# Two column groups of 384 instead of 512 and 256 for the products over all 768 tokens

## Chip, cores, metric

One core of one Trainium2 chip runs the kernel. The metric is the device time of one execution in microseconds; several executions are timed and the median is quoted.

## What is computed

A backbone of two layers over 512 latent tokens and 256 context tokens, model width 1024, in float32. Each layer runs three token mixers side by side (multi-head latent attention "MLA", a bidirectional gated linear recurrence "HGRN2", differential attention), merges them, and ends with a SwiGLU feed-forward network. The first layer computes all of it for all 768 tokens; the second needs from the context only what the latent tokens read of it.

```python
for l in range(2):
    ctx_out = l < 1
    h = x * (1 + sc1) + sh1                      # the same for ctx
    p = h @ w_in[l]                              # queries, keys, values, gates of all mixers
    y = (mla(p), hgrn2(p), diff_attention(p))    # latent tokens read context and latent tokens
    m = sum(sigmoid(h @ w_gate[i] + b_gate[i]) * (y[i] @ w_branch[i]) for i in range(3))
    x = post_norm(x, g1 * (m @ w_o))
    h2 = x * (1 + sc2) + sh2
    x = post_norm(x, g2 * ((silu(h2 @ w1a) * (h2 @ w1b)) @ w_ff2))
    # for ctx the same again, in the first layer only
```

## The kernel before

**Products.** Activations lie with features on the partitions and tokens along the free axis, split into a high and a low part (`h[0]`, `h[1]`); a weight tile of 128 output features is loaded, split the same way (`split_w`, line 380: ACT copies the high part `wh`, DVE subtracts for the low part `wl`), and each product is made of three matmuls per block of 128 input features (`mm3`, line 482): `wh`·`h` high, `wh`·`h` low, `wl`·`h` high. `fm_groups` (line 495) does this for a list of column groups `(offset, width)`: for each group it takes one PSUM bank, runs through the blocks, and calls `evac`, which brings the bank to SBUF. `GX = (256, 512)` are the latent tokens, `GC = (0, 256)` the context; a product over all 768 tokens runs GX and then GC. For a weight with 8 blocks that is 24 matmuls of 512 columns and 24 of 256.

**Jobs.** Such a product of one weight tile is a job. `win_jobs` (line 990) makes the 32 jobs per layer of the input projection (names dq, dk, dv of the differential attention, ff, fb, hq, hi, hg of the recurrence), `merge_jobs` (line 1557) the 8 gates and 8 branch products of each mixer, `ff1_jobs` (line 1778) the 44 products of the FFN's first half. Jobs stand in one list and run in its order. A job of the branch products waits for its mixer and for the differential attention (`Need(f"y{l}_2")` in `bran`).

**Order of the work.** The order of every engine's instructions is fixed when the program is built. The attentions and the recurrence are chains of short steps on PE, ACT and DVE (`mla` line 1016, `diff` line 1163, `hgrn` line 1374). `weave` (line 453) lays them between the jobs: where a chain yields `At(t)`, the time at which its next input will be ready by the cost table in `Clock.note` (line 199), it puts steps of the current job in front, until its count of PE's time has come near `t`. A step is six matmuls (two blocks of input features) of one group. In the first layer that list begins, beside the mixers, with the input projection and six gates of the first merge (lag 6 in `merge_jobs`); the first branch product can't be placed before the differential attention has ended. In the second layer it is the same.

**Tiles of names.** `b` and `S` are PSUM tiles (one bank, two banks), `wh`, `wl` and `wr` the split and the raw weights, `h` the activations, `s` and `k` tiles of 768 columns (the mixers' operands among them), `ident` the identity for transposes, `colv` columns of biases and gains, `ac` the FFN's gate.

```python
    def fm_groups(self, wt, nk, rhs, groups, evac, m=P, needs=None):
        for gi, (o, n) in enumerate(groups):
            if needs:
                yield Need(needs[gi])
            ps = self.bank()
            for k in range(nk):
                lh, ll = wt(k)
                rh, rl = rhs(k, o, n)
                self.mm3(ps[:m, :n], lh, ll, rh, rl, k == 0, k == nk - 1)
                if k % 2 == 1 and k != nk - 1:
                    yield 6 * mmcost(n)
            evac(ps, o, n)
            yield (6 if nk % 2 == 0 else 3) * mmcost(n)

```

Of the kernel before, what the change touches and what calls it, by code (L numbers as in the profile page):

```python
# [19 lines left out]
NK = 8  # L20
TX, TC, T = 512, 256, 768
XO = TC
# [10 lines left out]
MODJ = 2  # L33
O_HQ, O_FF, O_FB, O_HI, O_HG, O_DQ, O_DK, O_DV = 416, 928, 1440, 1952, 2464, 2976, 3488, 4000
GX, GC = (XO, TX), (0, TC)
XT = [2, 3, 4, 5]
CT = [0, 1]

# [231 lines left out]
class Kern:  # L270
# [529 lines left out]
    def mod_half(self, key, t, xo, g, hx, eng):  # L800
        nc = self.nc
        cx = 0 if t in XT else 1
        A, B = self.ab[key]
# [37 lines left out]
    def b1_tile(self, l, t):  # L841
        nc = self.nc
        first = not self.b1q
        isx = t in XT
        c0 = 0 if (isx or l == 0) else 256
# [144 lines left out]
    def win_jobs(self, l, names):  # L990

        nc = self.nc
        offs = dict(hq=O_HQ, ff=O_FF, fb=O_FB, hi=O_HI, hg=O_HG, dq=O_DQ, dk=O_DK, dv=O_DV)
        for nmj, j in names:
            ctxn = l == 0 or nmj in ("ff", "fb", "hi", "dk", "dv")
            groups = [GX, GC] if ctxn else [GX]
            park = self.dram([P, T])
            self.win[nmj, j] = park
            w = self.I["w_in"][l][:, offs[nmj] + j * P: offs[nmj] + (j + 1) * P]

            def body(job, nmj=nmj, j=j, groups=groups, park=park, ctxn=ctxn):
                s = self.slab()

                def evac(ps, o, n):
                    if o == XO:
                        nc.scalar.copy(s[:, o:o + n], ps[:, :n])
                    else:
                        nc.vector.tensor_copy(s[:, o:o + n], ps[:, :n])
                yield from self.fm_body(NK, self.hrhs(self.h), groups, evac, needs=[f"hx{l}", f"hc{l}"])(job)
                o = 0 if ctxn else XO  # L1010
                nc.sync.dma_start(park[:, o:], s[:, o:])
                self.done.add(f"win{l}_{nmj}{j}")
            self.add(Job(body, self.load_fm(w, NK), 1024))


    def mla(self, l):
# [6 lines left out]
        for h in range(8):  # L1023
            tiles += [(h, t, 6) for t in XT]
            if l == 0:
# [137 lines left out]
    def diff(self, l):  # L1163
# [3 lines left out]
        for h in range(4):  # L1167
            tiles += [(h, t, 6) for t in XT]
            if l == 0:
# [387 lines left out]
    def merge_jobs(self, l, br, seq):  # L1557
        nc, I = self.nc, self.I
        o0 = 0 if l == 0 else XO
        groups = [GX, GC] if l == 0 else [GX]  # L1560
        st = {}

        gates, brans = [], []
# [214 lines left out]
    def ff1_jobs(self, l):  # L1778
        nc, I = self.nc, self.I
        full = l == 0  # L1780
        groups = [GX, GC] if full else [GX]
        first = groups if full else [(XO, 256), (XO + 256, 256)]
        needs = [f"h2x{l}", f"h2c{l}"] if full else [f"h2a{l}", f"h2x{l}"]
        self.act = [None] * NFF
        every, self.every = self.every, 0
        for j in range(NFF):
            if j == MODJ:
                self.every, self.tick = every, 0.0
            st = {}

            def gate(job, j=j, st=st):
                def evac(ps, o, n):
                    st["g", o] = self.fp.tile([P, TX], F32, tag="ac", bufs=4, name=self.nm("ac"))
                    nc.scalar.activation(st["g", o][:, :n], ps[:, :n], AF.Silu)
                if j == 0:
                    st["late"] = self.fm_body(NK, self.hrhs2, first[1:], evac, needs=needs[1:])(job)
                yield from self.fm_body(NK, self.hrhs2, groups if j else first[:1], evac, needs=None if j else needs)(job)

            def up(job, j=j, st=st):
                a = self.slab()  # L1800
                self.act[j] = a

                def evac(ps, o, n):
                    nc.vector.tensor_tensor(a[:, o:o + n], st["g", o][:, :n], ps[:, :n], ALU.mult)
                if "late" in st:
                    job.defer = True
                    yield from self.fm_body(NK, self.hrhs2, first[:1], evac)(job)
                    yield from st["late"]
                    yield from self.fm_body(NK, self.hrhs2, first[1:], evac)(job)
                else:  # L1810
                    yield from self.fm_body(NK, self.hrhs2, groups, evac)(job)
                if j == NFF - 1:
                    self.done.add(f"act{l}")
            w = I["w_ff1"][l]
            self.add(Job(gate, self.load_fm(w[:, j * P:(j + 1) * P], NK), 1024))
            self.add(Job(up, self.load_fm(w[:, FF + j * P:FF + (j + 1) * P], NK), 1024))
# [24 lines left out]
def build(ctx, tc, I, out):  # L1841
# [4 lines left out]
    for t in range(6):  # L1846
        res[t] = I["ctx"][0, t * P:(t + 1) * P] if t < 2 else I["x"][0, (t - 2) * P:(t - 1) * P]
    order = XT + CT

# [9 lines left out]
    def start0(xin):  # L1859
# [3 lines left out]
        for g in range(2):  # L1863
            for blk in ((2, 0), (3, 1))[g]:
                yield Need(f"mod0_{blk}")
            for i, t in enumerate(XT):
                hx = K.fp.tile([P, TX], F32, tag="ac", bufs=4, name=K.nm("ac"))
# [178 lines left out]
```

## Time and profile before

| | |
|---|---|
| median of 3 runs | 2987.1 us (2985.87 to 2991.09) |
| profiled execution | 2997.48 us |
| its span, first to last instruction | 2995.7 us |
| mean granted TensorE clock | 0.964 of full speed |
| busy: PE, DVE, ACT, POOL | 2759.8, 1729.5, 1271.7, 273.0 us |

The span is the profiled execution's; the profiled execution as a whole took 0.35% longer than the median. Busy time of PE counts a matmul from its start to a modelled end, and matmuls overlap: what one costs in a dense stretch is the distance from its start to the next one's start, which the timeline gives. On a timeline row an instruction that is repeated without a gap stands once, with its count behind the x; in brackets stands how long the engine was idle before it and what ended that.

The stages: the first layer's MLA runs from about 160 to 445 us, its differential attention to 734, its recurrence to 980, the rest of the merge to 1080, the output projection and a normalisation to 1220, the FFN's first half to 1570, its second half, a normalisation and the second layer's first products to 1877; the second layer's MLA to 2092, its differential attention to 2293, its recurrence and merge to 2530, its FFN to the end.

### The profile page before, as it was taken

The page shows a single profiled execution, that of the slowest core. Times are in us where ns is not written, and L with a number is a line of the kernel's source. Part 1 is how long each engine was busy: PE and PEld are TensorE (multiplying, and loading weights), DVE is VectorE, ACT ScalarE, POOL GpSimd, SP SyncE. Part 2 cuts the span into 40 slices and gives each one's busy share as a digit, 9 for nine tenths or more (in the row PEclk, how much of TensorE's full clock was granted, in tenths as well). Part 3 has the DMA queues.
Part 4 walks back from the last instruction along what each step waited for, and adds up shares of the span by engine and source line. Part 5 has one row for each costly group of instructions (what it writes and reads, how often), then busy time and mean ns, then how long its engine had stood idle before and what let it go on. Part 6 is the DMA issues. An engine that isn't in the chain of part 4 may idle for free. (4 is left out here: it accounts for less than half of the span.)

```text
span 2995.7 us, 38612 instructions
## 1 busy us (share of the span) xinstructions
PE 2759.8 (92%) x14899; PEld 2327.7 (78%) x14899; DVE 1729.5 (58%) x2776; ACT 1271.7 (42%) x2321; POOL 273.0 (9%) x223
## 2 busy tenths in 40 slices
PE   6999989887999996999999989999989998799997
PEld 2888777766888885888888767888877887688875
DVE  4566656655876267555543566665665766622235
ACT  3545545576333224334432355444555453322222
POOL 1000000000000004333320120000000000300002
PEclk8999999988999998999999999999999999799998
DMA  6333353422432354353433354323332543333331
GB/s 216 99 115 93 110 150 125 139 62 86 139 121 90 106 188 132 121 155 118 150 105 120 106 184 112 93 89 120 106 110 85 174 129 132 115 99 99 106 127 70
DMA packets 345519, 359.11 MB, mean 120 GB/s; under 512 B 31114, under 2 KB 263044, under 8 KB 345336
## 3 DMA queue, kind: packets, MB, share of 16 engines
q1 hardware_dynamic: 343144, 351.84, 37.4%
q10 hardware_dynamic: 1680, 4.42, 0.4%
q8 instruction: 117, 1.92, 0.3%
q14 instruction: 66, 0.54, 0.1%
q0 software_dynamic: 512, 0.39, 0.0%
HBM read 298.10 MB, written 58.49 MB: 119 GB/s over the span
## 5 line engine op out<-in xcount | busy, mean ns | idle before, releaser
L106 PE MATMUL b<-h,wh 128*128 128x512 f32 (+1 forms) x5152 | 1372.9, 355 | 52.8 <-DVE h L106 15.3
L106 PEld LDWEIGHTS b<-h,wh 128*128 128x128 f32 x5152 | 905.9, 192 | 185.0 <-DVE h L106 16.4
L106 PE MATMUL b<-h,wl 128*128 128x512 f32 (+1 forms) x2576 | 905.9, 352 | 0.0
L106 DVE TENSOR_TENSOR wl<-wr,wh 128x1024 fp32r<-128x1024 f32 (+1 forms) x384 | 478.1, 1250 | 603.3 <-ACT wh L106 602.4
L106 ACT CAST wh<-wr 128x1024 fp32r<-128x1024 f32 (+1 forms) x384 | 379.8, 995 | 419.1 <-PE b L106 326.8
L106 PEld LDWEIGHTS b<-h,wl 128*128 128x128 f32 x2576 | 493.3, 191 | 65.1
L106 POOL TENSOR_TENSOR sm<-sm,mhalf 128x1 f32<-128x1 f32 (+3 forms) x80 | 56.4, 705 | 2439.6 <-DVE sm L106 2439.6
L106 ACT ACTIVATE s<-S,sm 128x768 f32<-128x768 f32 (+1 forms) x170 | 135.4, 797 | 336.2 <-DVE sm L106 288.9
L106 PE MATMUL S<-wh,ac 128*128 128x512 f32 x512 | 174.0, 404 | 17.5 <-DVE ac L106 11.5
L106 PE MATMUL b<-ident,s 128*128 128x128 f32 (+3 forms) x687 | 111.5, 277 | 70.4 <-ACT s L106 28.4
L106 PE MATMUL b<-k,wh 128*128 128x512 f32 (+1 forms) x576 | 165.4, 375 | 9.8 <-ACT k L106 9.1
L106 DVE TENSOR_TENSOR k<-b,k 128x512 fp32r<-128x512 f32 (+1 forms) x136 | 84.9, 627 | 134.7 <-ACT k L106 134.6
L106 PEld LDWEIGHTS b<-ident,s 128*128 128x128 f32 (+3 forms) x687 | 81.3, 142 | 92.9 <-ACT s L106 37.0
L106 PE MATMUL S<-k,k 96*128 96x512 f32 (+2 forms) x576 | 137.3, 341 | 12.6 <-DVE k L106 12.1
L106 DVE TENSOR_REDUCE sm<-S 128x1 f32<-128x768 f32 (+1 forms) x160 | 132.8, 842 | 18.7 <-PE S L106 18.4
L106 POOL TENSOR_TENSOR ln<-ln,wr 128x512 f32<-128x512 f32 x84 | 119.5, 1424 | 222.4 <-issue 161.5
L106 PEld LDWEIGHTS S<-wh,ac 128*128 128x128 f32 x512 | 97.2, 192 | 45.4 <-DVE ac L106 16.8
L106 PEld LDWEIGHTS b<-k,wh 128*128 128x128 f32 x576 | 103.5, 195 | 30.3 <-ACT k L106 11.7
L106 PEld LDWEIGHTS S<-k,k 96*128 96x128 f32 (+1 forms) x576 | 100.3, 191 | 33.8 <-DVE k L106 18.9
L106 PE MATMUL S<-k,s 128*128 128x128 f32 (+2 forms) x704 | 123.9, 298 | 1.3 <-ACT s L106 0.9
L106 ACT ACTIVATE wr<-wr,cact 128x512 f32<-128x512 f32 x84 | 59.9, 723 | 143.2 <-DVE ln L106 116.9
L106 ACT ACTIVATE ac<-b 128x512 f32<-128x512 f32 (+1 forms) x67 | 34.9, 520 | 191.7 <-PE b L106 191.6
(177 smaller groups left out, 3845.3 us busy)
## 6 DMA issues: line engine op xcount, KB each, us to landing
wr<-in_w_ff_dram SPq DMA_DIRECT2D x154, 512.0 KB
wr<-in_w_mod_dram SPq DMA_DIRECT2D x96, 512.0 KB
d<-s SPq DMA_DIRECT2D x88, 384.0 KB
wr<-in_w_in_dram SPq DMA_DIRECT2D x64, 512.0 KB
s<-d SPq DMA_DIRECT2D x80, 384.0 KB
wr<-in_w_gate_dram SPq DMA_DIRECT2D x48, 512.0 KB
wr<-in_w_branch_dram SPq DMA_DIRECT2D x48, 256.0 KB
wr<-in_w_o_dram SPq DMA_DIRECT2D x24, 512.0 KB
```

Of the source, the lines that this page charges most:

```text
L106: return getattr(getattr(self.clock.nc, self.eng), op)(*a, **k)
```

## The change

The products over all 768 tokens run as two groups of 384 columns, `HALVES = [(0, 384), (384, 384)]`, where they ran as 512 and 256. This holds for 29 of the first layer's 32 input projections (not dq, dk, dv of head 0), for the 20 of the second layer that read the context as well (ff, fb, hi, dk, dv), for the first layer's 24 gates and 24 branch products, and for 42 of its 44 products of the FFN's first half (not tile 0). Both groups of an input projection now wait for the context's activations (`hc`), where the first group waited for the latent ones (`hx`). In their `evac` ACT copies the second half and DVE the first; before, ACT copied 512 columns and DVE 256.

```diff
--- before.py
+++ after.py
@@ -33,6 +33,7 @@
 MODJ = 2
 O_HQ, O_FF, O_FB, O_HI, O_HG, O_DQ, O_DK, O_DV = 416, 928, 1440, 1952, 2464, 2976, 3488, 4000
 GX, GC = (XO, TX), (0, TC)
+HALVES = [(0, T // 2), (T // 2, T // 2)]
 XT = [2, 3, 4, 5]
 CT = [0, 1]
 
@@ -993,20 +994,23 @@
         offs = dict(hq=O_HQ, ff=O_FF, fb=O_FB, hi=O_HI, hg=O_HG, dq=O_DQ, dk=O_DK, dv=O_DV)
         for nmj, j in names:
             ctxn = l == 0 or nmj in ("ff", "fb", "hi", "dk", "dv")
+            needs = [f"hx{l}", f"hc{l}"]
             groups = [GX, GC] if ctxn else [GX]
+            if ctxn and (l, nmj, j) not in ((0, "dq", 0), (0, "dk", 0), (0, "dv", 0)):
+                groups, needs = HALVES, needs[1:] * 2
             park = self.dram([P, T])
             self.win[nmj, j] = park
             w = self.I["w_in"][l][:, offs[nmj] + j * P: offs[nmj] + (j + 1) * P]
 
-            def body(job, nmj=nmj, j=j, groups=groups, park=park, ctxn=ctxn):
+            def body(job, nmj=nmj, j=j, groups=groups, needs=needs, park=park, ctxn=ctxn):
                 s = self.slab()
 
                 def evac(ps, o, n):
-                    if o == XO:
+                    if o:
                         nc.scalar.copy(s[:, o:o + n], ps[:, :n])
                     else:
                         nc.vector.tensor_copy(s[:, o:o + n], ps[:, :n])
-                yield from self.fm_body(NK, self.hrhs(self.h), groups, evac, needs=[f"hx{l}", f"hc{l}"])(job)
+                yield from self.fm_body(NK, self.hrhs(self.h), groups, evac, needs=needs)(job)
                 o = 0 if ctxn else XO
                 nc.sync.dma_start(park[:, o:], s[:, o:])
                 self.done.add(f"win{l}_{nmj}{j}")
@@ -1557,7 +1561,7 @@
     def merge_jobs(self, l, br, seq):
         nc, I = self.nc, self.I
         o0 = 0 if l == 0 else XO
-        groups = [GX, GC] if l == 0 else [GX]
+        groups = HALVES if l == 0 else [GX]
         st = {}
 
         gates, brans = [], []
@@ -1778,8 +1782,8 @@
     def ff1_jobs(self, l):
         nc, I = self.nc, self.I
         full = l == 0
-        groups = [GX, GC] if full else [GX]
-        first = groups if full else [(XO, 256), (XO + 256, 256)]
+        groups = HALVES if full else [GX]
+        first = [GX, GC] if full else [(XO, 256), (XO + 256, 256)]
         needs = [f"h2x{l}", f"h2c{l}"] if full else [f"h2a{l}", f"h2x{l}"]
         self.act = [None] * NFF
         every, self.every = self.every, 0
```

Counted in PE's order, 3048 matmuls of 512 columns and 3048 of 256 become 6096 of 384, of which 288 and 288 are branch products (24 jobs of 12 each); the other 2760 pairs are 115 jobs of 24 pairs. The number of matmuls is the same, and so are all the other engines' instructions but for ACT's table loads (33 before, 37 in the change).

On PE in the first layer's FFN, at the border of a gate job's two groups (`b` the group's bank, `h` the activations, `wh` and `wl` the split weight), before:

```order
L106 MATMUL b_11704<-h_9931,wh_11562 128x512
L106 MATMUL b_11704<-h_9932,wh_11562 128x512
L106 MATMUL b_11704<-h_9931,wl_11563 128x512
L106 MATMUL b_11744<-h_9931,wh_11562 128x256
L106 MATMUL b_11744<-h_9932,wh_11562 128x256
L106 MATMUL b_11744<-h_9931,wl_11563 128x256
```

and in the change, at the same place:

```order
L107 MATMUL b_11704<-h_9931,wh_11562 128x384
L107 MATMUL b_11704<-h_9932,wh_11562 128x384
L107 MATMUL b_11704<-h_9931,wl_11563 128x384
L107 MATMUL b_11744<-h_9931,wh_11562 128x384
L107 MATMUL b_11744<-h_9932,wh_11562 128x384
L107 MATMUL b_11744<-h_9931,wl_11563 128x384
```

Nothing moved here; the second group is as wide as the first.

On PE at the end of the second layer's differential attention, up to the first branch product (`b<-k,wh`), before (`b<-h,w` are gate jobs; `b<-ident,s` is the last transpose of the attention):

```order
L106 MATMUL b_20075<-h_13834,wh_19937 128x512
L106 MATMUL b_20075<-h_13833,wl_19938 128x512
L106 MATMUL b_20075<-h_13833,wh_19937 128x512
L106 MATMUL b_20075<-h_13834,wh_19937 128x512
L106 MATMUL b_20075<-h_13833,wl_19938 128x512
L106 MATMUL b_20131<-ident,s_20097 128x128
L106 MATMUL b_20164<-k_20152,wh_20013 128x512 x2
L106 MATMUL b_20164<-k_20152,wl_20014 128x512
L106 MATMUL b_20164<-k_20155,wh_20013 128x512 x2
```

and in the change:

```order
L107 MATMUL b_20044<-ident,s_19999 128x128
L107 MATMUL b_20044<-k_19673,k_19970 128x256 x12
L107 MATMUL b_20076<-ident,s_20020 128x128 x4
L107 MATMUL S_18198<-ident,s_20020 128x128 x2
L107 MATMUL b_20087<-ident,s_20060 128x128
L107 MATMUL b_20087<-k_19673,k_20032 128x256 x12
L107 MATMUL b_20111<-ident,s_20102 128x128
L107 MATMUL b_20111<-k_19673,k_20075 128x256 x12
L107 MATMUL b_20135<-ident,s_20126 128x128
L107 MATMUL b_20164<-k_20152,wh_19788 128x512 x2
L107 MATMUL b_20164<-k_20152,wl_19789 128x512
L107 MATMUL b_20164<-k_20155,wh_19788 128x512 x2
```

The gate jobs' matmuls that stood between the attention's last steps are gone from there: they stand earlier, between the steps of the MLA and of the first tiles.

Counted in PE's order, with "fill" for the matmuls of input projections, gates and modulation rows that stand between the mixers' steps:

| stretch of PE's order | fill before | fill in the change |
|---|---|---|
| first layer: first scores of the MLA to first scores of the differential attention | 476 of 512, 426 of 256 | 888 of 384, 48 of 512 |
| first layer: the scores that begin at 680.87 us, to the first branch product | 60 of 512, 54 of 256 | 18 of 384, 4 of 512 |
| second layer: first scores of the MLA to first scores of the differential attention | 396 of 512, 336 of 256 | 726 of 384, 108 of 512 |
| second layer: the scores that begin at 2227.83 us, to the first branch product | 162 of 512 | 42 of 512 |

## Rows read from the trace of the kernel before

**Rows 1.** Page, busy time per engine: us (share of the span) and instructions.
```profile
PE 2759.8 (92%) x14899; PEld 2327.7 (78%) x14899; DVE 1729.5 (58%) x2776; ACT 1271.7 (42%) x2321; POOL 273.0 (9%) x223
```

**Rows 2.** Windows: stage, its us, then busy us per engine, granted clock, DMA.
```profile
160.00:445.00 285.00, 267.73 (x1652) 232.33 (x1651) 176.75 (x325) 137.24 (x277) 0.00 (x0) 0.98 0.37 110
...
445.00:680.00 235.00, 202.00 (x1186) 170.68 (x1185) 144.11 (x287) 139.91 (x275) 9.24 (x17) 0.96 0.35 110
...
680.00:734.00 54.00, 39.86 (x235) 31.83 (x233) 26.27 (x65) 35.67 (x76) 3.80 (x7) 0.86 0.19 61
...
980.00:1080.00 100.00, 100.00 (x578) 88.02 (x578) 39.63 (x56) 28.08 (x41) 0.00 (x0) 1.00 0.35 114
...
1220.00:1570.00 350.00, 348.81 (x2000) 301.43 (x1999) 189.97 (x204) 135.51 (x192) 115.61 (x81) 1.00 0.41 125
...
1877.00:2092.00 215.00, 211.49 (x1318) 188.15 (x1317) 135.64 (x235) 104.58 (x204) 0.00 (x0) 1.00 0.33 97
...
2092.00:2227.00 135.00, 124.29 (x710) 108.54 (x709) 92.92 (x171) 74.26 (x157) 4.90 (x9) 0.95 0.38 115
...
2227.00:2293.00 66.00, 57.78 (x309) 48.24 (x308) 32.77 (x68) 40.42 (x80) 3.80 (x7) 0.99 0.21 61
```

**Rows 3.** Timeline, PE, inside a gate job of the first FFN: start, us, instruction.
```profile
1338.37 0.63 PE L106 MATMUL b<-h,wh 128*128 128x512 f32 x2
...
1341.12 0.62 PE L106 MATMUL b<-h,wh 128*128 128x512 f32 x2
...
1343.84 0.40 PE L106 MATMUL b<-h,wh 128*128 128x256 f32 x2
...
1344.19 0.40 PE L106 MATMUL b<-h,wh 128*128 128x256 f32 x2
...
1345.27 0.40 PE L106 MATMUL b<-h,wh 128*128 128x256 f32 x2
```

**Rows 4.** Timeline, PE: other widths of matmul, and 256 columns of a branch job.
```profile
786.04 0.39 PE L106 MATMUL b<-k,wh 128*128 128x256 f32 x2
...
786.73 0.38 PE L106 MATMUL S<-s,s 128*128 128x128 f32 x2
...
1812.15 4.64 PE L106 MATMUL S<-s,h 128*128 128x416 f32 x24
...
1816.63 0.60 PE L106 MATMUL b<-ident,s 128*128 128x128 f32 x4
...
1828.48 2.69 PE L106 MATMUL S<-s,h 128*128 128x160 f32 x23
```

**Rows 5.** Timeline, PE: first and last instruction of two stretches, one per layer.
```profile
680.87 0.39 PE L106 MATMUL S<-k,k 128*128 128x512 f32 x1
...
733.98 0.79 PE L106 MATMUL b<-k,wh 128*128 128x512 f32 x1 [1.40 <-ACT k L106]
...
2227.83 0.44 PE L106 MATMUL S<-k,k 128*128 128x512 f32 x1
...
2292.34 0.50 PE L106 MATMUL b<-k,wh 128*128 128x512 f32 x1 [1.95 <-ACT k L106]
```

**Rows 6.** Timeline, PE, ACT and DVE: one tile of the second layer's differential attention.
```profile
2252.06 0.50 PE L106 MATMUL S<-k,k 128*128 128x512 f32 x1 [1.76 <-DVE k L106]
...
2258.26 1.28 ACT L106 ACT_TABLE_LOAD   x1
...
2259.55 0.69 ACT L106 ACTIVATE s<-b,colv 128x512 f32<-128x512 f32 x1
...
2260.14 1.04 ACT L106 CAST wh<-wr 128x1024 fp32r<-128x1024 f32 x1
...
2261.07 0.59 ACT L106 CAST k<-b 128x512 fp32r<-128x512 f32 x1
...
2261.21 1.23 DVE L106 TENSOR_TENSOR wl<-wr,wh 128x1024 fp32r<-128x1024 f32 x1 [4.14 <-ACT wh L106]
...
2263.42 0.50 PE L106 MATMUL S<-k,k 128*128 128x512 f32 x1 [2.03 <-DVE k L106]
```

## The prediction

> **What bounds the kernel now.** I read the page's busy times first: PE is busy for 2759.8 us of the span and no other engine for more than 1729.5 [rows 1]. An average hides stages, so the second view is the table by stage [rows 2]: busy PE is the whole stretch in the merge's rest (100.00 of 100) and nearly all in the first FFN half (348.81 of 350), and the second layer's MLA leaves PE idle for 3.5 us of 215. There, what PE saves is time saved. In the differential attentions it is not so: in the first layer PE is idle for 33.0 us of 235 and then 14.1 of 54, where ACT is busy for 35.67; in the second for 10.7 of 135 and 8.2 of 66. There the chain of steps over PE, ACT and DVE sets the pace, and the jobs between its steps are fill. The third view is the timeline, for what a matmul costs.
>
> **The price of a width.** In a gate job of the first FFN the 24 matmuls of 512 columns run from 1338.37 to 1343.84, 5.47 us; the last twelve of them take 2.72 us, 0.2267 each [rows 3]. Those of 256 columns take 1.08 us for nine, 0.120 each, and the first three 0.35 us, 0.117 [rows 3]. A group of 24 of them is 2.88 us, the job 8.35.
>
> Half of 0.2267 is 0.113, so a 256 costs 0.007 more than its columns. Why? 160 columns take 2.69 us for 23, 0.117 each at most, and six 256s of a branch job take 0.69 us, 0.115 each [rows 4]. If price were a constant plus columns, the line through 0.120 and 0.2267 would give 160 columns 0.080. They cost nearly as much as 256 do, so something besides the columns sets a floor of up to 0.12 per matmul: each has a weight load of its own. The 512s that follow a group of 256s also pay for it: the first twelve take 2.75 us, the last twelve 2.72 [rows 3].
>
> The trace has no matmul of 384 columns on `h`. Its price is bounded below by columns alone, 0.75 x 0.2267 = 0.170, and above by that line, 0.173. 416 columns took 4.48 us for 24, 0.187 each [rows 4], which is on the line (0.1867) and 1.5% over columns alone (0.184); but those have other operands. I take 0.170, from the 512s with the same operands, well above the floor. A job becomes 48 x 0.170 = 8.16 us: 0.19 less.
>
> 115 jobs by 0.19 are **21.9 us**: 42 FFN jobs 8.0, 18 gates behind the first layer's attentions 3.4, 29 projections and 6 gates in front of them 6.7, 20 projections in the second layer 3.8. The 288 branch pairs already run their 256s at 0.115 [rows 4], 0.002 over columns alone: at most 0.6 us, taken as nothing.
>
> A rule speaks against this. The Trainium skill (TensorE: Matmul & The Clock Gate, Back-to-back issue gap) makes a warm matmul its columns over 2.4 GHz plus 2.5 ns, by which 512 + 256 and 384 + 384 cost the same and the 21.9 us would be nothing. The same page (LDWEIGHTS) puts a load of 128 columns at 107 ns, under the 109 ns of a 256, so it would see no floor here. The rows put the 256 at 0.120, and I go by them.
>
> **What moves.** The order is laid by the program's own count of time. Six matmuls of 512 or of 256 were a large or a small step; now all steps are alike, and in the MLA more of them go between the chain's steps. In the second layer's MLA the fill was 396 x 0.2279 (5.47/24) + 336 x 0.120 = 130.6 us; it becomes 726 x 0.170 + 108 x 0.2279 = 148.0 us, 17 more in a stage that was full. The chain moves later there, and the list of jobs ends earlier: it is empty until the first branch product, which needs the differential attention done.
>
> At that end the second layer loses 120 of 162 fill matmuls, 27.3 us, out of a stretch of 64.5 us [rows 5]. In the first layer 60 x 0.2279 + 54 x 0.120 = 20.2 us become 18 x 0.170 + 4 x 0.2279 = 4.0, 16.2 us fewer, out of 53.1 [rows 5]. Together 43.5 us that now stand earlier, where PE is mostly full.
>
> How much shorter do the ends get? If PE set the pace, by all of it; if the chain did, by nothing. One tile of that end shows the mix [rows 6]: from scores to scores 11.36 us, with 24 fill matmuls, 5.5 us, in it (before 2240 to 2252 there were 30). The next tile's scores wait for DVE, which waits for ACT's copy `k<-b` at 2261.07. In front of that copy ACT loads a table (1.28), runs the gate's sigmoid (0.69) and converts the next weight (1.04): 2.81 us from 2258.26 to 2261.07 that exist only because a gate job runs there. The copy ends at 2261.66, but DVE is in that weight's low part until 2262.44: 0.8 more. Without fill a tile is 3.6 us shorter of 5.5, a share of 0.65. The last steps behind the tiles are pure chain, so I take 0.6: the ends give 26.1 us and keep **17.4**.
>
> In the first layer what comes forward does not all cost time, since PE had idle time to fill. Net of the cheaper price, 16.2 - 6.7 = 9.5 us come forward there, into stages with 17.3 and 33.0 us of idle time [rows 2]. Bounds nothing and 9.5; I take half, **4.8 us**. In the second layer's MLA, with 3.5 us idle, I take nothing.
>
> **Small edits.** Waiting for the context in both groups costs nothing: those jobs stand behind jobs that need products of the context already (the three that do not are left out); were it not so, a group of 5.47 us would be late once per layer. DVE copies 128 columns more and ACT 128 fewer in 49 jobs; by the conversion of 1024 columns in 1.23 us [rows 6] that is 0.15 us each, 7.5 us spread over MLA stages where DVE is busy for 176.75 of 285 and 135.64 of 215 [rows 2]: hidden. Were DVE late, the chain's next softmax would wait by that 0.15. ACT's four more table loads, 5.1 us, replace nothing on PE; they lie in tiles that keep their fill, and I leave them to the range. DMAs are the same in number and size.
>
> **The sum.** -21.9 + 17.4 - 4.8 = -9.3 us. It is made on the profiled execution, 2997.48 us, whose span is 2995.7; taken off the median of 2987.1, which is 0.35% less, it gives **2978 us**.
>
> **The rivals.**
> *The whole price arrives.* The chain's ends shrink by all that leaves them, and only PE's count is left: -21.9, 2965 us; with some idle time filled besides, 2963. For it: even in the ends PE is busy for 39.86 of 54 and 57.78 of 66 [rows 2]. Against: the 3.6 of 5.5 above, and the idle time in both.
> *The ends keep most of it (slower).* PE runs out of jobs in the last tiles of both differential attentions and waits for the chain. It turns the sign where the ends shrink by under 39% of the 43.5 us (43.5 x 0.61 = 26.7 = 21.9 + 4.8). If only a quarter comes back, 32.6 is kept: with no idle time filled, +10.7, 2998 us. For it: in 680 to 734 ACT is busy for two thirds, PE for three quarters, so neither is the bound but the chain's length. Against: the table load, the sigmoid and the conversion go with the fill.
> *384 columns cost what the line says.* At 0.1733 a job takes 8.32 us and 115 save 3.5 us, while the order still moves: -3.5 + 17.4 - 4.8 = +9.1, 2996 us. For it: the 416s. Against: the 160s, and the 512s on the same operands. By the Trainium skill's rule above the saving would be nothing at all, and the time 3000.
> *The change does not do what it says:* excluded, the order has 6096 matmuls of 384 columns.
>
> **How the numbers follow.** Forecast 52%, whole price 16%, ends keep most 17%, the line's price 15%. A measurement of this kernel can tell about 0.2%, 6 us, from no change. Of the forecast four fifths lie beyond -6 us (42%), the rest within 6 (10%); the whole price is faster (16%); of the rival ends 10% are slower and 7% within; of the line's price 8% slower, 7% within. Faster 0.58, same 0.24, slower 0.18. The range goes from the whole price with idle time filled, 2963, to the ends that keep three quarters, 2998; beyond it I leave 2 in 10. The forecast alone would be 2969 to 2986, from ends that shrink by 80% or by 40%.
>
> **What would show it.** In the first FFN the timeline has 384s on `h` 0.170 apart, and 42 jobs make that stage 8 us shorter: over 0.172 and the price is wrong. The second layer's MLA is longer by about 15 us (17 less its share of idle time). The end of its differential attention, from the scores of the third-last tile to the first branch product, has 120 fill matmuls fewer and is 16 us shorter, not 27 and not 5, with PE idle for longer than now; in the first layer 10 us shorter. A clock below 2.4 GHz in those ends, which is granted at 0.86 already in the first layer's [rows 2], would make them worse than I reckon. If the MLA does not grow, the fill was not in PE's way, and if the ends do not shrink, the time is 3000 or more.

## The result

The change takes 3014.06 us (median of 4 runs, 3011.55 to 3017.37), the kernel before beside it 2986.53 (2985.87 to 2991.09): a ratio of 1.009, 95% interval 1.0072 to 1.0107, so 27 us slower. Forecast was 2978, within 2963 to 2998.

The profiled execution of the change took 3011.55 us, 2.5 under its median; that of before lay 10.4 over its own, so the two traces differ by 14 us where the medians differ by 27. A second profile of before (first experiment) took 2993.26 us. Lengths below are between the same steps of the chains in each trace, and the last lines of the argument rest on timed medians.

The page of the change, busy time per engine:

```profile
PE 2762.9 (92%) x14899; PEld 2462.0 (82%) x14899; DVE 1734.5 (58%) x2776; ACT 1271.3 (42%) x2325; POOL 272.5 (9%) x223
```

Against [rows 1] only the weight loads moved, 2327.7 to 2462.0 us, for the same 14899 of them. ACT has the four more instructions, table loads. PE is nearly as busy as before (3.1 us more) in a span that is 14.1 us longer: most of what was added is time in which PE stands. Where it stands is a matter of stages. The windows of the change, cut at the chain steps that cut [rows 2] (stage, its us, then busy us of PE, PEld, DVE, ACT, POOL, the granted clock, DMA):

```profile
160.00:451.00 291.00, 280.05 (x1729) 262.82 (x1730) 181.41 (x330) 139.19 (x284) 0.00 (x0) 0.99 0.36 113
451.00:691.00 240.00, 207.35 (x1190) 191.28 (x1190) 146.00 (x286) 143.03 (x281) 9.20 (x17) 0.94 0.34 106
691.00:742.00 51.00, 28.06 (x135) 22.91 (x133) 21.95 (x58) 23.45 (x59) 3.78 (x7) 0.74 0.09 31
1877.00:2107.00 230.00, 229.48 (x1420) 219.70 (x1419) 139.29 (x238) 105.33 (x208) 0.00 (x0) 1.00 0.34 104
2107.00:2247.00 140.00, 129.07 (x709) 114.22 (x708) 94.65 (x170) 85.86 (x167) 4.88 (x9) 0.95 0.36 109
2247.00:2307.00 60.00, 37.42 (x189) 31.95 (x188) 27.22 (x63) 29.71 (x68) 3.78 (x7) 0.83 0.05 17
```

The second layer's MLA was 215 us with PE idle for 3.5; it is 230 with PE idle for 0.5. The end of its differential attention was 66 us with PE idle for 8.2; it is 60 with PE idle for 22.6. The first layer's end was 54 with PE idle for 14.1; it is 51 with 22.9. Fill left the ends, and the ends hardly got shorter.

The marks of both ends, in PE's timeline of the change, stand against [rows 5]:

```profile
691.13 0.39 PE L107 MATMUL S<-k,k 128*128 128x512 f32 x1
...
742.38 0.69 PE L107 MATMUL b<-k,wh 128*128 128x384 f32 x1 [1.40 <-ACT k L107]
...
2247.41 0.39 PE L107 MATMUL S<-k,k 128*128 128x512 f32 x1
...
2306.59 1.52 PE L107 MATMUL b<-k,wh 128*128 128x512 f32 x2 [0.96 <-ACT k L107]
```

The first end went from 53.1 to 51.2 us, the second from 64.5 to 59.2. And the price of 384 columns, in PE's timeline inside the first FFN, 78 matmuls from the first of these rows to the second:

```profile
1289.79 0.51 PE L107 MATMUL b<-h,wh 128*128 128x384 f32 x2
...
1303.31 0.51 PE L107 MATMUL b<-h,wh 128*128 128x384 f32 x2
```

13.52 / 78 = 0.1733 us, the line through 256 and 512 to the last digit, not 0.170.

### The profile page after: what moved, and what is told of

The parts are those of the page before. It is cut to its first block, busy times and chain, and to the rows that moved or that the text cites. A ratio compares the mean times of both kernels' runs of the same rounds, so it can differ in the third digit from the quotient of the medians.

```text
span 3009.8 us, 38588 instructions
## 1 busy us (share of the span) xinstructions
PE 2762.9 (92%) x14899; PEld 2462.0 (82%) x14899; DVE 1734.5 (58%) x2776; ACT 1271.3 (42%) x2325; POOL 272.5 (9%) x223
## 5 line engine op out<-in xcount | busy, mean ns | idle before, releaser
L107 PE MATMUL b<-h,wh 128*128 128x384 f32 (+2 forms) x5152 | 1404.6, 354 | 54.9 <-ACT h L107 16.7
L107 PEld LDWEIGHTS b<-h,wh 128*128 128x128 f32 x5152 | 938.2, 191 | 118.8 <-ACT s L107 18.0
L107 PE MATMUL b<-h,wl 128*128 128x384 f32 (+2 forms) x2576 | 903.7, 351 | 0.0
L107 PEld LDWEIGHTS b<-h,wl 128*128 128x128 f32 x2576 | 491.3, 191 | 26.9
L107 PE MATMUL b<-ident,s 128*128 128x128 f32 (+3 forms) x687 | 113.0, 279 | 77.1 <-DVE s L107 24.6
L107 PE MATMUL b<-k,wh 128*128 128x384 f32 (+1 forms) x576 | 166.4, 369 | 8.9 <-ACT k L107 8.5
L107 PE MATMUL S<-k,k 96*128 96x512 f32 (+2 forms) x576 | 137.5, 341 | 13.0 <-DVE k L107 12.9
L107 DVE TENSOR_REDUCE sm<-S 128x1 f32<-128x768 f32 (+1 forms) x160 | 132.7, 841 | 17.1 <-PE S L107 17.0
L107 ACT COPY s<-b 64x256 f32<-64x256 f32 (+5 forms) x160 | 74.0, 472 | 100.5 <-PE b L107 96.7
```

The lines of the kernel that those rows point to most:

```text
L107: return getattr(getattr(self.clock.nc, self.eng), op)(*a, **k)
```

## The experiments

This table gathers what the traces of the runs show in which fill moves. Each cell is the fill in a stretch, counted in the order of PE and priced at 0.2267, 0.1733 and 0.120 us, and behind the slash the stretch's length. L1 and L2 are the layers. The marks: a product ahead of the MLA's scores, at 131 us (L1), or those scores (L2); first scores of the differential attention; the scores that begin the end, as in [rows 5]; first branch product. Counted this way, the first row of the table of fill ahead of the prediction does not reach from mark to mark: between the first layer's first scores of the MLA and of the differential attention stand 500 of 512 and 450 of 256 before, and 978 of 384 and 52 of 512 in the change. The prediction uses the other rows, which are right. The expectations of experiments 5 and 7 begin the first layer's differential attention at an earlier mark, with 7 us of fill ahead of its first scores; that moves fill between two cells and leaves their sums as they are.

| run | L1 MLA | L1 diff. | L1 end | L2 MLA | L2 diff. | L2 end |
|---|---|---|---|---|---|---|
| before (as on record) | 173.5 / 313.6 | 131.3 / 235.6 | 20.1 / 53.1 | 130.1 / 214.5 | 75.8 / 135.7 | 36.7 / 64.5 |
| before again | 173.5 / 311.7 | 131.3 / 236.8 | 20.1 / 53.1 | 130.1 / 214.4 | 75.8 / 135.6 | 36.7 / 64.4 |
| the change | 188.6 / 321.8 | 132.3 / 239.8 | 4.0 / 51.2 | 150.3 / 229.6 | 80.9 / 140.5 | 9.5 / 59.2 |
| order of the change, 512 and 256 | 189.2 / 325.1 | 132.6 / 233.4 | 3.1 / 50.6 | 150.0 / 231.5 | 80.9 / 140.6 | 9.5 / 59.3 |
| order of before, 384 | 172.2 / 326.9 | 132.3 / 245.6 | 20.4 / 52.1 | 131.3 / 222.7 | 75.8 / 134.9 | 36.7 / 64.4 |
| only L1's projections 384 | 188.6 / 323.3 | 134.0 / 241.0 | 2.3 / 51.5 | 130.1 / 214.5 | 75.8 / 132.8 | 36.7 / 64.4 |
| only L1's merge 384 | 173.5 / 313.6 | 142.2 / 245.7 | 9.2 / 51.5 | 130.1 / 214.4 | 75.8 / 133.9 | 36.7 / 64.5 |
| only L2's projections 384 | 173.5 / 313.0 | 131.3 / 235.4 | 20.1 / 53.1 | 150.3 / 229.6 | 80.9 / 141.5 | 9.5 / 59.3 |
| change, 0.5 in L2 | 188.6 / 322.9 | 132.3 / 242.6 | 4.0 / 51.1 | 127.6 / 213.3 | 89.4 / 145.5 | 25.8 / 56.5 |
| change, 0.5 in both | 178.3 / 333.8 | 122.0 / 226.1 | 24.6 / 54.8 | 127.6 / 213.3 | 89.4 / 144.6 | 25.8 / 57.4 |
| before, 0.5 in L1 | 157.9 / 303.5 | 120.0 / 220.3 | 47.0 / 68.5 | 130.1 / 214.4 | 75.8 / 135.6 | 36.7 / 64.4 |
| change, idle ends filled with empty matmuls | 188.6 / 324.5 | 132.3 / 242.8 | 4.0 (+28.1) / 48.8 | 150.3 / 229.7 | 80.9 / 142.2 | 9.5 (+24.5) / 57.3 |

**1. Before again** (`e_base`), an edit of no instruction, to see how far two profiles of one kernel differ.

> The kernel before, run once more for a second profile: between 2985 and 2998 us. If its span lies near 2984, about 12 us under the first profile's 2995.7, the profile shown of before is a long one, and the stages in which the two profiles differ are those in which an execution varies by itself. If it lies near 2996, profiling itself lengthens this kernel.

2993.26 us, 4.2 under the first profile, all of it up to the second layer's MLA: the first MLA is 1.9 us shorter, its differential attention 1.2 longer, the stretch from the first branch product to the second layer's MLA 2.4 shorter (1143.7 to 1141.3). In the table a first-layer cell of one trace is good to about 2 us.

**2. Width and order taken apart** (`e_w512_order_after`, `e_w384_order_before`). The program's count of time is told a width that is not issued; the order of the instructions of PE, ACT, DVE and POOL is then the other kernel's, instruction for instruction in the traces, with the groups of 512 and 256 in the places of the two 384s, or the reverse:

```diff
+def planned(groups, gi, n):                 # order of before, 384 columns issued
+    return (512, 256)[gi] if groups is HALVES else n
...
+            p = planned(groups, gi, n)
...
-                    yield 6 * mmcost(n)
+                    yield 6 * mmcost(p)
```

> The reverse: groups of 512 and 256 as before, counted by the planner as two of 384, so that every engine's instructions stand in the order of the change. ORDER: as slow as the change, ratio 1.009 to 1.012. WIDTH: as before, 1.000.

> Two groups of 384 everywhere as in the change, but the program's planner counts them as 512 and 256, so every engine's instructions stand in the order of before. If the order is what lengthens the change (theory ORDER), this is as fast as before or a little faster: 115 jobs of 48 matmuls at 0.1733 against 8.35 us a job, 3 us less, ratio 0.999 (0.996 to 1.001). If the width itself costs (theory WIDTH: more weight loads in flight, other copies), it is at the change's 1.009. If the price were 0.170, as predicted, 0.993.

The order of the change with 512 and 256 columns took 3012.93 us, ratio 1.0077 (1.0065 to 1.009): nearly the whole loss without a single 384; the interval overlaps the change's. The other one took 3028.88, ratio 1.013 (1.0113 to 1.0146), slower than either kernel, which neither theory had. Its excess is in the MLAs, 13 to 15 and 8 us, in the first differential attention, 9 to 10, and in the stretch from the first branch product to the second layer's MLA, 8 to 10. PE's timeline shows one piece of it, in the first layer's MLA (start, us, instruction, and in brackets the idle time before it and what ended it):

```profile
399.56 0.64 PE L111 MATMUL b<-h,wh 128*128 128x384 f32 x2 [2.04 <-ACT s L111]
400.02 0.50 PE L111 MATMUL b<-h,wl 128*128 128x384 f32 x1
400.31 0.84 PE L111 MATMUL b<-h,wh 128*128 128x384 f32 x2
...
401.27 0.84 PE L111 MATMUL b<-h,wh 128*128 128x384 f32 x2
...
402.23 0.84 PE L111 MATMUL b<-h,wh 128*128 128x384 f32 x2
402.88 0.52 PE L111 MATMUL b<-h,wl 128*128 128x384 f32 x1
...
405.55 0.52 PE L111 MATMUL b<-h,wh 128*128 128x384 f32 x2
406.09 0.52 PE L111 MATMUL b<-h,wh 128*128 128x384 f32 x2
```

After a wait of 2.04 us the 384s come 0.96 / 3 = 0.320 us apart, which is 384 columns at 1.2 GHz; from 405.55 they are back near the 0.173 of 2.4 GHz. The granted clock of that stretch (behind the POOL column) is 0.50:

```profile
400.31:403.19 2.88, 2.88 (x10) 2.88 (x10) 1.75 (x5) 0.35 (x1) 0.00 (x0) 0.50 0.02 6
```

In the whole stretch of the first MLA in the table, PE stands for 26.9 us (19.1 and 18.7 in the two traces of before), and the granted clock is at its lower level for 20.5 us (10.2 and 6.8). Work takes twice as long there, so 10 to 14 us more of it are worth 5 to 7, an estimate; with 8 us more of standing that makes the 13 to 15. For the other stretches this was not worked out. What follows is only this: an order laid for one pair of widths is not good for the other, and the change's order, laid for its own width, still loses 27.

**3. The FFN alone** (`e_ff1_only`), where no chain's steps stand between the jobs:

```diff
-        groups = [GX, GC] if full else [GX]
-        first = groups if full else [(XO, 256), (XO + 256, 256)]
+        groups = HALVES if full else [GX]
+        first = [GX, GC] if full else [(XO, 256), (XO + 256, 256)]
```

> Only the FFN's first half of the first layer runs as two groups of 384; its 42 jobs stand where PE is busy throughout. At 0.1733 a job of 48 saves 0.03 us, 1.3 us in all: ratio 0.9996. At 0.170 it would be 8.0 us: 0.9973.

2987.33 us beside 2990.33, ratio 0.999 (0.9981 to 0.9999). 42 jobs at 48 x 0.1733 = 8.32 instead of 8.35 us are worth 1.3 us, at the predicted 8.16 they would be 8.0; the interval, 0.3 to 5.7 us, holds the first only. The traces say the same of the stage itself: from the first to the last matmul of its 42 jobs it takes 367.0 us in both traces of before and 366.4 in this run and in the change, 0.6 us less and not 8.

**4. The second layer's projections alone** (`e_win1_only`):

```diff
+            if ctxn and (l, nmj, j) not in ((0, "dq", 0), (0, "dk", 0), (0, "dv", 0)) and l == 1:
+                groups, needs = HALVES, needs[1:] * 2
```

> Only the second layer's 20 projections are cut 384 and 384; everything of the first layer is as before. The order of the second layer's attentions is then that of the change: 150.3 us of fill in its MLA instead of 130.1, 16.3 instead of 36.7 at the end of its differential attention. PLACE (fill that stands in the MLA costs its own time there, because PE is idle for 3.4 us of 214 there, and the end gives little of it back): the MLA is 15 us longer, the end 3 to 4 us shorter, the whole 14 to 17 us over before: about 3005. EVEN (the loss is one of the whole order, the first layer's share being as large as its share of the jobs): 20 of 115 jobs, +4: about 2994. PREDICTION (the end gives back 0.6 of what leaves it): +4.

3008.26 us beside 2990.82, ratio 1.0059 (1.0047 to 1.0071): 17.6 us, the largest part of the loss, from 20 of 115 jobs. The windows of this run for the second layer's MLA, differential attention and end:

```profile
1873.00:2103.00 230.00, 229.49 (x1419) 219.76 (x1418) 139.27 (x238) 105.25 (x208) 0.00 (x0) 1.00 0.35 104
2103.00:2244.00 141.00, 129.42 (x710) 114.98 (x709) 94.19 (x170) 85.91 (x167) 4.88 (x9) 0.95 0.36 109
2244.00:2303.00 59.00, 38.80 (x185) 32.67 (x183) 26.77 (x62) 28.97 (x66) 3.79 (x7) 0.75 0.05 14
```

15 us more in the MLA, 5 to 6 in the attention, 5 back in the end: the change's second layer to within 1 us.

**5. The fill put back, at the change's widths** (`e_room_change_l1`, `e_room_change_both`). One number of `weave` in the MLA:

```diff
-                while self.ck.at["tensor"] < r.t - 0.1 and self.dstep() is not None:
+                while self.ck.at["tensor"] < r.t - self.room and self.dstep() is not None:
...
+                K.room = (0.1, 0.5)[l]               # both: (0.5, 0.5)[l]
                 yield from K.mla(l)
+                K.room = (0.1, 0.1)[l]
                 yield from K.diff(l)
```

> The change, with one number more: in the second layer's MLA a step of fill is only put ahead of a wait while at least 0.5 us of the planned wait are left, not 0.1. All widths are the change's. The MLA's fill falls from 150.3 us to 127.6 (714 matmuls, before had 732), the differential attention's goes from 74.1 to 79.8 and its end's from 16.3 to 35.4. PLACE: the MLA is 15 to 17 us shorter than the change's, the rest of the attention 4 to 6 us longer: about 3002. WIDTH (384s in the MLA hold up the chain's matmuls, wherever the rest stands): the MLA keeps at least 10 of its 15 us, and the time stays at 3010 or above.

> The same number in both layers' MLAs. In the first layer the MLA's fill falls from 157.9 us to 145.5, the differential attention's from 139.4 to 122.0, the merge into its end rises from 8.2 to 28.7 (before had 25.1). PLACE: the first layer's MLA is 9 us shorter, its differential attention up to 10, its end 5 longer: 5 to 12 us under the run with the number in the second layer alone, about 2993, so that the loss of the change is gone with the change's widths. WIDTH: no better than 3005.

With the number in the second layer: 3000.03 us, ratio 1.0031 (1.0019 to 1.0043), 14 under the change. Its windows for the second layer's MLA, attention and end:

```profile
1880.00:2093.00 213.00, 209.11 (x1296) 197.25 (x1297) 135.10 (x234) 100.29 (x201) 0.00 (x0) 1.00 0.34 99
2093.00:2239.00 146.00, 137.73 (x775) 125.27 (x774) 96.80 (x176) 80.29 (x168) 4.88 (x9) 0.96 0.38 116
2239.00:2295.00 56.00, 45.84 (x255) 38.25 (x253) 29.55 (x64) 36.55 (x71) 3.78 (x7) 0.96 0.14 40
```

The MLA is at 213 us again, with 384s in it: their place cost the 15 us, not their width. From the MLA's scores to the first branch product the second layer takes 415 us, as before. The end, with 16.3 us more fill in it than in the change, is 2.7 shorter. With the number in both layers nothing more came: 3002.56 us (2994.16 to 3004.6), ratio 1.0033, where 2993 was expected. There the first layer's attention got 16.5 us shorter with 10.3 us less fill and its end 3.7 longer with 20.6 more, but its MLA got 11 us longer with 10 us less fill (the run with the number in the second layer alone has 322.9 us there). PE's waits in the two MLAs (waits in us in total, times, longest), first without and then with the number:

```profile
PE b L107 <- DVE k L107: 1.3, 1, 1.3
...
PE b L107 <- DVE k L107: 13.4, 5, 5.1
...
PE S L107 <- DVE k L107: 3.8, 3, 2.5
```

Without that fill PE waits for DVE's `k` for 17.2 us instead of 1.3, stands for 27.2 instead of 12.8 in all, and has the lower clock for 17.1 us instead of 6.8. So in the first layer's MLA less fill is not less time at 384 columns; why DVE is late there stays open. One candidate was not tried: the program's own cost table (`mmcost`, 0.000443 us per column, at least 0.118) has 384 columns at 0.170 where they take 0.1733, so its plan of the change runs ahead of the chip.

**6. The same at the widths of before** (`e_room_before_l0`), to ask whether the ends of before have room too: `K.room = (0.5, 0.1)[l]` ahead of `K.mla`.

> The kernel before, with its own widths of 512 and 256, and the 0.5 in the first layer's MLA. There the MLA's fill falls from 144.5 us to 129.5, the differential attention's from 131.3 to 120.0, its end's rises from 25.1 to 43.3, and 9 us go behind it. PLACE (fill is nearly free in the end of the differential attention, whatever its widths): the MLA is 11 us shorter, the differential attention 5, the end 6 longer and the recurrence 9 longer: 0 to 8 us under before, about 2986. FULL END (the end is filled beyond what the chain leaves): the end is longer by all of the 18, 2990 to 2998.

2979.94 us beside 2990.82, ratio 0.9959 (0.9943 to 0.9975): faster than both kernels, and by more than expected: the attention gave 15 to 17 us, not 5. The windows of its first layer's differential attention and of the 68 us from the scores that begin the end to the first branch product:

```profile
434.00:655.00 221.00, 191.57 (x1123) 159.59 (x1123) 141.88 (x286) 124.03 (x261) 9.74 (x18) 0.96 0.37 113
655.00:723.00 68.00, 63.38 (x383) 53.26 (x382) 35.59 (x75) 48.51 (x91) 3.24 (x6) 0.99 0.36 115
```

PE is busy for 63.38 of 68 us at a granted clock of 0.99, where before had 39.86 of 54 at 0.86. This end is 15 us longer for 27 us more fill, while 27 us less in the MLA and the attention shorten those by 8 to 10 and 15 to 17. So the end's room is bounded: up to 24.6 us of fill it takes 49 to 55 us, from there to 47.0 it pays about 0.6 of what is added.

**7. The two other parts alone** (`e_win0_only`, the condition of experiment 4 with `l == 0`, without the three jobs that the change leaves out; `e_merge_only`):

```diff
-        groups = [GX, GC] if l == 0 else [GX]
+        groups = HALVES if l == 0 else [GX]
```

> Only the first layer's 29 projections are cut 384 and 384. Fill in that layer's MLA up to its second-last head 157.9 us instead of 144.5, in the last tiles 23.5 instead of 29.0, in the differential attention 141.1 instead of 131.3, in its end 7.4 instead of 25.1. PLACE (the end gives back an eighth to a sixth of what leaves it, the attentions take theirs nearly whole): 17.7 us come forward, 3 come back, some idle time in front of the differential attention is filled: 6 to 12 us over before, 2997 to 3003. PREDICTION: 0.6 of 17.7 comes back, half of the rest is absorbed: +1 to +4, 2992 to 2995.

> Only the first layer's merge (24 gates, and the branch pairs behind them) is cut 384 and 384. The MLA stays as before; 10.9 us of fill come forward from the end of the differential attention into it (142.2 instead of 131.3, and 13.4 instead of 25.1). PLACE: the differential attention is 9 to 11 us longer, the end 1 to 2 shorter, the 18 gates and the branches behind cost as before: +7 to +10, about 2999. PREDICTION: the end is 7 us shorter, idle time (33 us there) takes half of what comes: -2 to +1.

2998.27 us beside 2990.02, ratio 1.0032 (1.002 to 1.0044), and 2993.05, ratio 1.0013 (1.0004 to 1.0022). The first is as the place of the fill has it. The second is a half miss: the differential attention grew by 9 to 10 us and the end gave back 1.6, as expected, but from the first branch product to the second layer's MLA this trace is 5 us shorter than the second one of before (1136.3 against 1141.3), so 3 us are left, not 7 to 10. In that stretch the granted clock is at its lower level for 64.9 us in this trace and for 74.7 in that one; half of the difference, 4.9 us as an estimate, would cover the 5. It varies there without any change of the merge too: 74.0 us in the first trace of before, 58.0 in experiment 9. So how much of the merge's part is its own and how much is chance stays open. By parts: +17.6 (second layer's projections), +8.3 (first layer's), +3.0 (merge), -3.0 (FFN): +25.9, against 27 for the whole.

**8. The idle ends filled with empty matmuls** (`e_warm_ends`): the change, and wherever the job list is empty during a differential attention, four more matmuls of 512 columns into a bank that nobody reads.

```diff
+        ps, hh = self.bank(), self.h[0]
+        for k in range(4):
+            self.nc.tensor.matmul(ps[:, :512], hh[:, k, :P], hh[:, k + 4, :512], start=k == 0, stop=k == 3)
...
-                while self.ck.at["tensor"] < r.t - 0.1 and self.dstep() is not None:
-                    pass
+                while self.ck.at["tensor"] < r.t - 0.1:
+                    if self.dstep() is None and not self.warmup():
+                        break
```

> The change, with matmuls that compute nothing used added wherever the list of jobs is empty while a differential attention waits: 124 of 512 columns in the first layer's end (28.1 us by 0.2267), 92 in the second's (20.9 us), 16 behind it (3.6 us); no ACT or DVE work comes with them. Question: does PE's idling itself, with the granted clock of 0.82 and 0.84 in the two ends, keep the ends from shrinking? CLOCK: the chain's own matmuls run at 2.4 GHz again, and the second layer's end is up to 6 us shorter (its time beside fill and idle is 30.8 us in the change, 24.3 before), the first's up to 4: 3003 to 3008. CHAIN (ACT's and DVE's steps set the pace, PE's state does not matter): 3010 to 3016. PREDICTION (0.6 of any fill in the ends is paid): 0.6 x 49 = 29 us more, about 3042. FULL: all of 52 us more, 3065.

3013.85 us (3005.0 to 3016.76), ratio 1.0072 (1.0057 to 1.0087): 52.6 us of PE work, and no time. The windows of the two ends:

```profile
697.00:746.00 49.00, 47.57 (x258) 39.62 (x256) 22.29 (x58) 24.12 (x60) 3.69 (x7) 0.99 0.10 32
2255.00:2313.00 58.00, 54.16 (x296) 45.58 (x294) 27.25 (x63) 29.95 (x68) 3.78 (x7) 1.00 0.05 15
```

PE is full at a granted clock of 0.99 and 1.00, where the change had 0.74 and 0.83, and the ends are 2.4 and 1.9 us shorter. So the clock of an idle PE costs about 2 us per end, less than I had allowed; at this amount of fill PE's time is not what the ends are made of.

**9. The best parts together** (`e_room_before_ff1`): experiment 6 with experiment 3.

> The kernel before with the 0.5 us in the first layer's MLA, and the first FFN's 42 jobs cut 384 and 384, the only part of the change that measured no worse than before. Sum of the two parts as measured (0.9959 and 0.999): 0.9949, about 2976. If the two do not add up: 2980.

2974.99 us beside 2990.02, ratio 0.995 (0.9938 to 0.9963): 15 us faster than before and 39 than the change.

## Why the prediction was wrong

Two terms of the sum failed, by 18 to 19 us each: the price of a 384, which made -21.9 us of what is -3.5, and the share that the ends give back, which made 17.4 us kept of what is 36.3.

**The price: 0.170 was wrong, 0.1733 right.** The step was "I take 0.170, from the 512s with the same operands, well above the floor". Both bounds were on the page, 2% apart, but the term multiplies them by 5520 matmuls: 21.9 us at one end, 3.5 at the other. The row that should have decided is 416 columns at 0.187 [rows 4], the only width between, and it lay on the line. A cost of 13.3 ns per matmul beside its columns (0.2267 less 512 at 2.4 GHz) fits 256, 384, 416 and 512 (not 160, at 0.117); I had read the 256s' 0.120 as a floor instead. The third rival had this. The Trainium skill (TensorE: Matmul & The Clock Gate, Back-to-back issue gap) has the same form, columns over the clock plus a constant, by which two groups of 384 cost what 512 and 256 cost. The runs agree with that consequence, 48 x 0.1733 = 8.32 us against 24 x 0.3467 = 8.32, though not with its constant of 2.5 ns: the rows have 13.3.

**The MLA: right.** "Longer by about 15 us" in the second layer: 214.5 to 229.6 with 20.2 us more fill, and experiments 4 and 5 move it there and back. The step that PE idles too little there to hide fill holds: its idle time fell from 3.5 to 0.5 us.

**The ends: the share of 0.6 was wrong.** The ends were to give back 26.1 of 43.5 us; they gave 1.9 and 5.3, a share of 0.17, and kept 36.3 instead of 17.4. The second end, which the forecast begins at its third-last tile, begins at the fourth-last: four tiles' scores start in it. Its tiles show where my tile [rows 6] misled. One tile of the change with 12 fill matmuls (2258.69 to 2270.45, 11.76 us) and the next with none (to 2278.89, 8.44 us), PE, ACT and DVE:

```profile
2258.69 0.50 PE L107 MATMUL S<-k,k 128*128 128x512 f32 x1 [0.67 <-DVE k L107]
...
2262.70 0.39 PE L107 MATMUL b<-h,wl 128*128 128x512 f32 x1
...
2266.25 1.28 ACT L107 ACT_TABLE_LOAD   x1
2267.55 0.69 ACT L107 ACTIVATE s<-b,colv 128x512 f32<-128x512 f32 x1
2268.13 0.61 ACT L107 CAST wh<-wr 128x512 fp32r<-128x512 f32 x1
2268.64 0.59 ACT L107 CAST k<-b 128x512 fp32r<-128x512 f32 x1
...
2270.45 0.50 PE L107 MATMUL S<-k,k 128*128 128x512 f32 x1 [3.14 <-DVE k L107]
...
2275.58 0.90 ACT L107 ACTIVATE s<-S,sm 128x768 f32<-128x768 f32 x1
2276.47 0.58 ACT L107 CAST k<-b 128x512 fp32r<-128x512 f32 x1
...
2278.89 0.54 PE L107 MATMUL S<-k,k 128*128 128x512 f32 x1
```

I had the steps: behind the exponentials ACT spends 2.4 us on a gate's table load, sigmoid and weight before it copies `k<-b`, and in this pair the tile without them is 3.3 us shorter. But those steps come once per gate, not once per matmul. PE's last fill of this tile starts at 2262.70, and ahead of the next scores it waits 3.14 us for DVE's `k` all the same, which comes behind that copy. So the three tiles before the last stretch lost 42 of their 84 fill matmuls, 9.5 us, and got 4.1 us shorter, 2.9 of it in the tile that lost its gate (11.36 to 8.44). That the gate alone decides is not shown: in experiment 5 tiles with a gate and 24 to 30 fill matmuls took 10.3 to 10.6 us.

The larger error is the stretch behind the last scores. It is pure chain, as I wrote, but I gave it a share near that of the tiles: 78 of the 162 matmuls stood there. Before it was 2263.42 to 2292.34, 28.9 us with 17.7 of fill; now it is 2278.89 to 2306.59, 27.7 with none. Part of this is the clock, which the prediction named as a danger and did not price: the same stretch took 25.0 us with 36 fill matmuls (experiment 5) and 25.1 with empty ones at a granted clock near 1.00 (experiment 8), so 2.6 of the 27.7 us went with the lower clock of an idle PE.

**The absorbed 4.8 us: right in size.** In the first layer's MLA and differential attention there is 16.1 us more fill, and they are 12.3 us longer (13.0 by the second profile of before): 3 to 4 absorbed. Not where I looked, though: PE's idle time in the differential attention was 33.0 us of 235 [rows 2] and is 32.7 of 240, and the fill there is nearly the same (131.3 and 132.3 us). It came forward into the MLA, where PE's idle time fell from 19.1 to 12.9 us: the two longest waits of before, 3.9 and 4.4 us ahead of that attention, in the MLA's last tiles, are gone.

**Small edits.** The wait for the context, the copies and the four table loads are not seen as a loss in any stage; they were not tried by themselves, so this is not shown.

**The sum redone.** With the measured price and share: -3.5 + 36.3 - 4.8 = +28.0, measured +27. That it comes out so closely is partly luck. In the second layer 25.3 us of fill came into the MLA and the attention and made them 19.9 us longer, so 5.4 us more were absorbed, which the sum puts at nothing; and the stretch from the first branch product to the second layer's MLA is 6 to 9 us shorter in the change's trace, more than the price can give. The trace of the change is 14 and 18 us longer than the two of before, not 27; the rest lies between single executions and medians and is not placed in a stage. What I had kept as two rivals, the line's price and ends that keep most, are not alternatives: each says nothing against the other, and both came. Their joint case, some 3015 us, was in my own numbers and stood outside the range, because I gave each a price with the other at the forecast's value.

## What to carry to other kernels

Fill is worth what its stretch lacks. Before an edit that moves fill, split the program into stretches where PE is the bound (in the second layer's MLA each us of fill cost 0.7 to 0.75) and stretches where the chain is (in the ends it cost 0.17, until PE was nearly full), and price a move by the two slopes, not by a mean over a sample tile. The slopes hold where they were measured: in the first layer's MLA the same number of `weave` took 8 to 10 us off at the widths of before and added 11 at the change's. In a kernel whose list of jobs runs out before a chain-bound end, try holding fill back for that end: one number, 0.1 to 0.5, gave 11 us here at the widths of before, where the change of widths lost 27.

When a term multiplies a small difference by thousands of instructions, measure that difference or carry both ends through the sum; and rivals that can be true together need a case in which they are.

## What the runs showed of the hardware

Weight loads of 128 x 128 are charged with more busy time next to 384s (2462.0 us for 14899 in the change, 2463.5 with 384s in the order of before) than next to 512s and 256s (2327.7, and 2335.3 in the order of the change), while the matmuls of the first FFN keep their pace (366.4 and 367.0 us). So more busy time of PEld was no sign of a cost here. Behind a wait of 2.04 us PE had two matmuls at full clock and then ten at a granted clock of 0.50, about 0.32 us apart instead of 0.173, in a stage with a mean granted clock of 0.97. And 232 matmuls of 512 columns, 52.6 us of PE time, fitted into two ends of 51 and 59 us and made them shorter by 2.4 and 1.9.
